# Heads of 64 rows: one head on each half of the array's rows, into two banks, in place of keys on a diagonal with zeros

## The chip, the cores and the metric

One core of one Trainium2 chip. The metric is the device time of one execution in microseconds (us), as the median of several runs.

## The reference

A stack of two networks on 256 tokens of width 1024, all in float32. The first has two layers: a mixer (layer 0, "even": two attentions of 8 heads of 64; layer 1, "odd": 8 differential heads, each of two score maps over 64 features), a cross attention to a memory of 256 tokens with 4 heads of 64 ("mem"), and a gated feed-forward. The second has two layers of feed-forward, a mixer of three branches ("mix"), and feed-forward again. The branches are a neighborhood attention with 8 heads of 64, a gated linear attention with 4 heads of 64 keys, and a latent attention whose heads have 128 + 64 features. What the change touches is the products that sum over 64 features or over a chunk of 64 tokens:

```python
s = jnp.einsum('bqhd,bkhd->bhqk', qb, k).astype(jnp.float32) * scale   # d = 64
p = masked_softmax(s, ...)
o = jnp.einsum('bhqk,bkhd->bqhd', p.astype(v.dtype), v)
...
a = jnp.where(tri, jnp.einsum('bhnid,bhnjd->bhnij', qe, ke), 0.0)      # gated linear, d = 64
upd = jnp.einsum('bhncd,bhncv->bhndv', k_end, v)                       # c = a chunk of 64 tokens
```

## The kernel before

The tokens are two tiles of 128 (t = 0, 1). Weights stream from HBM in pieces of 128x1024 (`raw`), are split into a high and a low part by ScalarE and VectorE (`split`, L390 and L392) and multiply in three single-pass products (`mm3`, L399 to L401). The feed-forwards take most of the time and are not touched.

In the attentions the two heads of a pair p lie on the 128 rows of `qT[:, p]`, 64 each. `kpair` (two copies for a tile) writes the keys of the first head into rows 0 to 63 of a buffer `kb[:, p, 0]` and those of the second into rows 64 to 127 of `kb[:, p, 1]`; the other halves were set to zero by `begin` or `mem_slots` on GpSimd. One matmul over all 128 rows (L686) gives the scores of both heads side by side in one PSUM bank `ps_s`:

```python
mm(o, qT[:, p, q], kb(p)[:, :, :w], start=True, stop=not mask)
```

A float32 matmul is two passes on TensorE in the trace: one written instruction is two in the counts. `causal_units` cuts the attention into units of one or two pairs; a unit fills one of the two banks of `ps_s`. After a unit come the largest value (L626, VectorE), the exponential (L636, ScalarE), the division (L643), the transposes (L455, into `ps_t`), the copy to `PT`, and the product with the values, which has 64 output columns for a head, so that the two heads of a pair stand on the two halves of the array's columns (L858, L885, L1082, L1246).

The gated linear attention has the same zeros: in `vb` (values, one chunk on each half, L1415) and `kb` (keys of the two directions, L1439). The latent attention adds the 64 further features of two heads by L1325.

The order on each engine is fixed when the kernel is built, by a scheduler that fills the gaps of an attention with the projections that come next. An engine then works through its list in order. A `with self.chain()` block takes its transposes into `ps_t`; work outside takes `ps_u`. In `mem` the projection of the queries of a tile also takes a bank of `ps_s`.

Of the kernel before, what the change touches and what calls it, by code (L numbers as in the profile page):

```python
# [50 lines left out]
BUFS = {"tok": (3, 2), "half": (3, 2), "xn": (2, 1), "P": (3, 3), "PT": (3, 3)}  # L51
# [83 lines left out]
def pack_rpb(rpb):  # L135

    tok = np.arange(256)
    r, c = tok // 64, tok % 64
    c0 = np.clip(c - 8, 0, 48)
    ok = (c[None, :] >= c0[:, None]) & (c[None, :] < c0[:, None] + 16)  # L140
    dr = np.broadcast_to(r[None, :] - r[:, None] + 7, (256, 256))
    dc = np.where(ok, c[None, :] - c[:, None] + 15, 31)
    padded = np.full((8, 15, 32), NEG, np.float32)
    padded[:, :, :31] = rpb
    return np.ascontiguousarray(padded[:, dr, dc].reshape(4, 2, 2, 128, 256).transpose(0, 2, 3, 1, 4))
# [56 lines left out]
class Net:  # L202
# [67 lines left out]
    def begin(self, na, nr, nk=()):  # L270
# [4 lines left out]
        self.K = [self.slot("slot", F32).rearrange("p (a b n) -> p a b n", a=4, b=2) for _ in nk]  # L275
# [4 lines left out]
        for k, n in zip(self.K, nk):  # L280
            nc.gpsimd.memset(k[0:64, :n, 1], 0.0)
            nc.gpsimd.memset(k[64:128, :n, 0], 0.0)
# [373 lines left out]

    def flat(self, P):
        return P.rearrange("p n w -> p (n w)")
# [7 lines left out]
    def kpair(self, kb, k0, v, t):  # L666

        m = v.shape[1]
        s = slice(t * 128, t * 128 + v.shape[2])
        for i in range(2):  # L670
            h = slice(i * 64, (i + 1) * 64)
            self.evac(kb[h, k0:k0 + m, i, s], v[h])

    def causal_units(self):

        return [(0, 128, (0, 1)), (0, 128, (2, 3))] + [(1, 256, (p,)) for p in range(4)]

    def score_unit(self, unit, qT, kb, extra=None, mask=True):
# [3 lines left out]
        S = self.bank("s").rearrange("p (n w) -> p n w", w=w)  # L682
        q = slice(t * 128, (t + 1) * 128)
        for i, p in enumerate(prs):
            o = S[:, 2 * i:2 * i + 2]
            mm(o, qT[:, p, q], kb(p)[:, :, :w], start=True, stop=not mask)  # L686
            if extra:
                extra(o, p, w)
            if mask:
                mm(o[:, :, w - 128:], self.identb, self.causal[:, None, :].to_broadcast([128, 2, 128]), start=False,  # L690
                   stop=True)
        return S[:, :2 * len(prs)]
# [84 lines left out]
    def even(self, xT, finish, filler):  # L777
# [5 lines left out]
        kb2, kb = self.K  # L783
# [3 lines left out]
        def evk(t, ps):  # L787
            self.rope(hd(kk[t][:, 0:384]), hd(ps[:, 0:384]), t, 6)
            self.evac(kk[t][:, 384:416], ps[:, 384:416])
            self.kpair(kb2, 0, self.transposes(kk[t][:, 128:384], 2), t)  # L790
# [7 lines left out]
        with self.chain():  # L798
# [11 lines left out]
            nc.vector.tensor_scalar(fl, fl, 0.0, None, op0=ALU.min)  # L810
            for i in range(2):
                nc.vector.tensor_sub(self.lfm[:, :, i, i::2], fl[:, :, i::2], fa[:, :, i::2])
# [8 lines left out]
            for t in range(2):  # L821
# [17 lines left out]
                for u in self.causal_units():  # L839
# [3 lines left out]
                    PTs = []  # L843
                    for br in range(2):
                        S = self.score_unit(u, qT2, lambda p: kb2[:, br])
                        P, r = self.softmax(S)
                        r2 = self.sm(r.shape[-1])
                        nc.vector.tensor_mul(r2, r, gt[:, t, 8 + 8 * br + 2 * prs[0]:8 + 8 * br + 2 * prs[-1] + 2])
                        self.scaled(P, r2)
                        PTs.append(self.probsT(self.flat(P)))  # L850
                    for i, p in enumerate(prs):
                        for h in range(2):
                            o = O[h * 64:h * 64 + 64, p]
                            mm(o, self.vcbd[:, 2 * p + h], PcT[:, 0], start=True, stop=False)
                            for br in range(2):
                                for b in range(t + 1):
                                    c = 128 + br * 128 + h * 64
                                    mm(o, v5[:, b, c:c + 64], PTs[br][:, (2 * i + h) * (t + 1) + b], start=False,  # L858
# [5 lines left out]
        for j in range(2):  # L864
            self.projT(st, xT, lambda c, ps: self.kpair(kb, 2 * j + c, ps[:, None, :], 0))
# [6 lines left out]
        with self.chain():  # L872
            O = None
            for u in self.causal_units():
                t, w, prs = u
                S = self.score_unit(u, qT, lambda p: kb[:, p], bias)
                P, r = self.softmax(S)
                self.scaled(P, r)
                PT = self.probsT(self.flat(P))
                if prs[0] == 0:  # L880
                    O = self.bank("o").rearrange("p (k n) -> p k n", k=4)
                for i, p in enumerate(prs):
                    for h in range(2):
                        for b in range(t + 1):
                            mm(O[h * 64:h * 64 + 64, p], V[:, b, p * 128 + h * 64:p * 128 + h * 64 + 64],  # L885
                               PT[:, (2 * i + h) * (t + 1) + b], start=b == 0, stop=b == t)
# [77 lines left out]
    def odd(self, xT, finish, filler):  # L964
# [14 lines left out]
        for half in range(2):  # L979
            kb = self.K[half]  # L980
            qT = self.q4(2 * half)
            def evk(t, ps):
                tk = self.tile([128, 512], F32, "tok")
                self.rope(hd(tk), hd(ps), t, 8)
                self.kpair(kb, 0, self.transposes(tk, 4), t)
# [7 lines left out]
            with self.chain():  # L993

                units = self.causal_units()
                for i, (ua, ub) in enumerate(zip(units[::2], units[1::2])):
                    t = ua[0]
                    Pd = self.tile([128, 4, 128], F32, "tok").rearrange("p a b -> p (a b)")
                    for j, u in enumerate((ua, ub)):
                        w, prs = u[1:]  # L1000
                        P, r = self.softmax(self.score_unit(u, qT, lambda p: kb[:, p]))
                        r2 = self.sm(r.shape[-1])
                        nc.vector.tensor_scalar(r2, r, self.lamc, None, op0=ALU.mult)
                        for p in range(len(prs)):
                            a, b = P[:, 2 * p], P[:, 2 * p + 1]
                            d = Pd[:, j * 256 + p * w:j * 256 + (p + 1) * w]
                            nc.vector.tensor_scalar(b, b, r2[:, 2 * p + 1:2 * p + 2], None, op0=ALU.mult)
# [539 lines left out]
```

## Time and profile before

| | us |
|---|---|
| median of 3 runs | 2085.9 (2081.1 to 2088.89) |
| the profiled execution: its time / its span | 2088.63 / 2086.9 |
| TensorE busy in the span | 2032.0 |
| VectorE, ScalarE, GpSimd busy | 1401.0, 1175.3, 106.5 |
| mean granted TensorE clock | 0.993 of full |

The span runs from the first to the last instruction; 1.7 us lie around it. TensorE's busy time counts a matmul from its start to its end, also while the next one already streams, so the distance from one start to the next is what a matmul costs.

### The profile page before, as it was taken

Reading aid. Unit: us, or ns where it says so; the run is one execution under the profiler, and the core shown is the slowest. Engines: PE = TensorE matmul, PEld = TensorE weight load, DVE = VectorE, ACT = ScalarE, POOL = GpSimd, SP = SyncE. Lnnn points to the kernel's source line nnn. Section 1 sums busy time; section 2 is a strip of 40 time slices with the busy share of each in tenths; the row PEclk is TensorE's granted clock in tenths of the full one; section 3 lists DMA queues with packets and bytes.
Section 4 is the critical chain, followed back from the end, with each engine's and each line's share of the span. In section 5 each row is a group of like instructions: output and inputs, shape, how many; then the busy total and the mean of one; then the engine's idle time right before and its main releaser. Section 6 shows DMA issues by size and latency. Waiting matters only on the chain.

```text
span 2086.9 us, 30850 instructions
## 1 busy us (share of the span) xinstructions
PE 2032.0 (97%) x11094; PEld 1703.5 (82%) x11094; DVE 1401.0 (67%) x2909; ACT 1175.3 (56%) x2566; POOL 106.5 (5%) x189
## 2 busy tenths in 40 slices
PE   7998999999899999999999999999999999999999
PEld 6866888877688889887778888888888878889887
DVE  7766766578676667665768677666665677867663
ACT  6645665466465556554654557555654564556652
POOL 1000000100100000002101000000000200100000
PEclk9999999999999999999999999999999999999999
DMA  7505565443456546553443467554663444556650
GB/s 239 173 30 182 175 229 182 144 142 116 167 187 225 184 142 228 186 182 109 151 165 122 157 202 253 191 183 161 217 189 111 147 153 136 172 175 206 225 182 31
DMA packets 100473, 352.15 MB, mean 169 GB/s; under 512 B 12468, under 2 KB 12980, under 8 KB 100320
## 3 DMA queue, kind: packets, MB, share of 16 engines
q1 hardware_dynamic: 96912, 337.99, 49.6%
q0 software_dynamic: 3408, 12.20, 1.9%
q8 instruction: 87, 1.43, 0.3%
q14 instruction: 66, 0.54, 0.1%
HBM read 349.09 MB, written 1.05 MB: 168 GB/s over the span
## 4 chain that ended last, share of the span: by engine, by line
PE 90%; DVE 3%; DMA 3%; ACT 2%; issue 1%; POOL 0%; ACTq 0%; DVEq 0%
PE ps_a L401 11%; PE ps_a L399 10%; PE ps_a L400 10%; PE ps_s L410 8%; PE ps_s L408 5%; PE ps_o L399 4%; PE ps_o L401 4%; PE ps_o L400 4%; PE ps_u L410 4%; PE ps_t L410 4%; PE ps_s L401 3%; PE ps_s L399 2%; PE ps_s L400 2%; PE ps_u L408 2%; PE ps_t L408 2%; PE ps_s L686 2%
## 5 line engine op out<-in xcount | busy, mean ns | idle before, releaser
L392 DVE TENSOR_TENSOR ring<-raw,ring 128x512 fp32r<-128x512 f32 x724 | 466.4, 679 | 165.5 <-ACT ring L390 159.7
L390 ACT ACTIVATE ring<-raw 128x512 fp32r<-128x512 f32 x724 | 411.8, 617 | 191.1 <-PE ps_a L401 69.8
L392 DVE TENSOR_TENSOR slot<-raw,slot 128x512 fp32r<-128x512 f32 x548 | 356.0, 687 | 187.2 <-ACT slot L390 185.2
L390 ACT ACTIVATE slot<-raw 128x512 fp32r<-128x512 f32 x548 | 314.2, 622 | 165.9 <-PE ps_o L401 108.1
L399 PE MATMUL ps_a<-ring,XX 128*128 128x512 f32 (+3 forms) x544 | 213.2, 395 | 3.8 <-ACT XX L390 3.8
L400 PE MATMUL ps_a<-ring,XX 128*128 128x512 f32 (+3 forms) x544 | 212.9, 392 | 0.0
L401 PE MATMUL ps_a<-ring,XX 128*128 128x512 f32 (+3 forms) x544 | 212.5, 391 | 0.0
L410 PE MATMUL ps_s<-XX,slot 128*128 128x512 f32 x492 | 178.1, 393 | 0.0
L408 PE MATMUL ps_s<-XX,slot 128*128 128x256 f32 x552 | 145.5, 281 | 0.0
L399 PEld LDWEIGHTS ps_a<-ring,XX 128*128 128x128 f32 x544 | 102.7, 190 | 25.7 <-ACT XX L390 5.6
L401 PEld LDWEIGHTS ps_a<-ring,XX 128*128 128x128 f32 x544 | 103.1, 190 | 22.2 <-issue 4.0
L400 PEld LDWEIGHTS ps_a<-ring,XX 128*128 128x128 f32 x544 | 103.3, 190 | 19.7 <-issue 1.4
L408 PEld LDWEIGHTS ps_s<-XX,slot 128*128 128x128 f32 x552 | 103.7, 188 | 6.7
L410 PEld LDWEIGHTS ps_s<-XX,slot 128*128 128x128 f32 x492 | 92.4, 188 | 18.7
L410 PE MATMUL ps_s<-XX,ring 128*128 128x512 f32 x264 | 96.1, 393 | 0.0
L410 PE MATMUL ps_t<-XX,slot 128*128 128x512 f32 x258 | 93.3, 393 | 0.0
L432 POOL TENSOR_TENSOR sm<-sm,mhalf 128x1 f32<-128x1 f32 (+2 forms) x72 | 59.1, 822 | 655.7 <-DVE sm L429 355.8
L410 PE MATMUL ps_u<-XX,slot 128*128 128x512 f32 x234 | 84.2, 393 | 0.0
L399 PE MATMUL ps_s<-slot,XX 128*128 128x256 f32 x288 | 81.8, 285 | 2.3 <-ACT XX L390 2.3
L401 PE MATMUL ps_s<-slot,XX 128*128 128x256 f32 x288 | 81.9, 288 | 0.0
L400 PE MATMUL ps_s<-slot,XX 128*128 128x256 f32 x288 | 81.1, 283 | 0.0
L408 PE MATMUL ps_s<-XX,ring 128*128 128x256 f32 x312 | 79.8, 281 | 0.0
(442 smaller groups left out, 4726.5 us busy)
## 6 DMA issues: line engine op xcount, KB each, us to landing
raw<-f SPq DMA_DIRECT2D x264, 512.0 KB, 4.3
raw<-ffn SPq DMA_DIRECT2D x132, 512.0 KB, 4.4
raw<-win SPq DMA_DIRECT2D x52, 512.0 KB, 4.2
raw<-wgt SPq DMA_DIRECT2D x48, 512.0 KB, 4.2
raw<-od_in SPq DMA_DIRECT2D x24, 512.0 KB, 4.2
raw<-wbr SPq DMA_DIRECT2D x24, 512.0 KB, 3.4
raw<-ev_in SPq DMA_DIRECT2D x16, 512.0 KB, 4.5
raw<-wout SPq DMA_DIRECT2D x16, 512.0 KB, 4.0
```

Of the source, the lines that this page charges most:

```text
L390: a = nc.scalar.activation(hi, src, AF.Copy, scale=scale)
L392: b = nc.vector.tensor_tensor(lo, src, hi.bitcast(F32), op=ALU.subtract)
L399: mm(out, a[0], b[0], start=first, stop=False)
L400: mm(out, a[0], b[1], start=False, stop=False)
L401: mm(out, a[1], b[0], start=False, stop=last)
L408: mm(out[:, :256], w[1], self.XX[:, k, 0], start=False, stop=False)
L410: mm(out, w[0], self.XX[:, k], start=False, stop=last)
L432: self.pow = nc.gpsimd.tensor_tensor(r, v, self.mhalf[:, :n], op=ALU.pow).ins
L686: mm(o, qT[:, p, q], kb(p)[:, :, :w], start=True, stop=not mask)
```

## The change

A matmul now takes one head: 64 rows of queries and 64 rows of keys, on the upper half of the array's rows for the first head and on the lower half for the second. The two heads go to two banks of `ps_s`. A unit therefore holds both banks, has twice as many pairs, and softmax runs over a bank of one head. The key buffers lose their zeros and are copied once. The gated linear attention and the latent attention change in the same way. `mem` takes its query projection into `ps_a` or `ps_o`. The buffers `P` and `PT` grow from 3 and 3 to 4 and 5, for which a DMA scratch area is made smaller.

```diff
-BUFS = {"tok": (3, 2), "half": (3, 2), "xn": (2, 1), "P": (3, 3), "PT": (3, 3)}
+BUFS = {"tok": (3, 2), "half": (3, 2), "xn": (2, 1), "P": (4, 4), "PT": (5, 5)}
...
+    def probs(self, Ss, biases=(None, None)):
+
+        PTs = []
+        for S, bias in zip(Ss, biases):
+            P, r = self.softmax(S, bias)
+            self.scaled(P, r)
+            PTs.append(self.probsT(self.flat(P)))
+        return PTs
...
     def causal_units(self):
 
-        return [(0, 128, (0, 1)), (0, 128, (2, 3))] + [(1, 256, (p,)) for p in range(4)]
+        return [(0, 128, (0, 1, 2, 3)), (1, 256, (0, 1)), (1, 256, (2, 3))]
 
-    def score_unit(self, unit, qT, kb, extra=None, mask=True):
+    def score_unit(self, unit, qT, kT, extra=None, mask=True):
...
-        S = self.bank("s").rearrange("p (n w) -> p n w", w=w)
+        n = len(prs)
+        S = [self.bank("s")[:, :n * w].rearrange("p (n w) -> p n w", w=w) for _ in range(2)]
         q = slice(t * 128, (t + 1) * 128)
         for i, p in enumerate(prs):
-            o = S[:, 2 * i:2 * i + 2]
-            mm(o, qT[:, p, q], kb(p)[:, :, :w], start=True, stop=not mask)
+            for h in range(2):
+                r = slice(h * 64, h * 64 + 64)
+                mm(S[h][:, i], qT[r, p, q], kT(p)[r, :w], start=i == 0 or not mask, stop=not mask)
...
+    def weigh(self, O, V, PTs, prs, nb, c0=0):
+
+        for i, p in enumerate(prs):
+            for h in range(2):
+                for b in range(nb):
+                    c = c0 + p * 128 + h * 64
+                    self.nc.tensor.matmul(O[h * 64:h * 64 + 64, p], V[:, b, c:c + 64], PTs[h][:, i * nb + b], start=b == 0,
+                                          stop=b == nb - 1)
...
-                ps = self.bank("s")[:, :256]
+                ps = self.bank("ao"[t])[:, :256]
...
-                        U = self.bank("o").rearrange("p (h c v) -> p h c v", h=2, c=2)
-                        for j in range(2):
-                            h = 2 * g + j
-                            mm(U[:, j], E[:, h * 128:h * 128 + 128], vb[:, h, :, tq(t)], start=True, stop=True)
+                    U = [self.bank("o").rearrange("p (h v) -> p h v", h=4) for _ in range(2)]
+                    for h in range(4):
+                        hs = slice(h * 128, h * 128 + 128)
+                        for c in range(2):
+                            r = slice(c * 64, c * 64 + 64)
+                            mm(U[c][:, h], E[r, hs], V[r, t, hs], start=True, stop=True)
```

The scheduler's order moves with it. On TensorE, in the second attention of the even mixer (tile t = 1), a unit of one pair stood before as one matmul for both heads (`ps_s_167`) with its mask (L690):

```order
L401 MATMUL ps_a_319_1692<-ring_308_1659,slot_37_198 128x512
L686 MATMUL ps_s_167_911<-slot_38_199,slot_30_191 128x512
L690 LDWEIGHTS identb_216
L690 MATMUL ps_s_167_911<-causal_228,identb_216 128x2x128
L858 MATMUL ps_o_118_725<-PT_134_780,slot_30_191 64x128
```

and stands now as two stretches, `ps_s_158` of the first head and `ps_s_159` of the second, each with the two pairs and a mask (L692), with projections (L395 to L397) between them:

```order
L686 MATMUL ps_s_158_886<-slot_34_195,slot_30_191 128x256 x2
L692 LDWEIGHTS identb_211
L692 MATMUL ps_s_158_886<-causal_223,identb_211 128x2x128
L396 MATMUL ps_a_318_1699<-ring_305_1659,slot_38_199 128x512
L397 MATMUL ps_a_318_1699<-ring_305_1659,slot_38_199 128x512
...
L686 MATMUL ps_s_159_887<-slot_34_195,slot_30_191 128x256 x2
L692 LDWEIGHTS identb_211
L692 MATMUL ps_s_159_887<-causal_223,identb_211 128x2x128
```

The two heads no longer stand next to each other. In the first `mem` the scores of tile 1 stood on TensorE behind the twelve matmuls of the output projection of tile 0 (`ps_a_420` and `ps_a_421`; the last two of them here):

```order
L400 MATMUL ps_a_421_2149<-ring_401_2063,slot_393_2034 128x512
L401 MATMUL ps_a_421_2149<-ring_401_2063,slot_393_2034 128x512
L686 MATMUL ps_s_444_2238<-slot_40_213,slot_391_2032 128x512
L686 MATMUL ps_s_451_2261<-slot_40_213,slot_391_2032 128x512
L455 MATMUL ps_t_449_2250<-identf_88,P_445_2240 128x128 x4
```

and stand now behind two of them, with the heads in turn (`ps_s_443`, `ps_s_444`) and ten of the twelve still to come:

```order
L395 MATMUL ps_a_419_2155<-ring_398_2061,slot_392_2039 128x512
L396 MATMUL ps_a_419_2155<-ring_398_2061,slot_392_2039 128x512
L686 MATMUL ps_s_443_2245<-slot_39_209,slot_390_2037 128x256
L686 MATMUL ps_s_444_2246<-slot_39_209,slot_390_2037 128x256
L686 MATMUL ps_s_443_2245<-slot_39_209,slot_390_2037 128x256
L686 MATMUL ps_s_444_2246<-slot_39_209,slot_390_2037 128x256
L397 MATMUL ps_a_419_2155<-ring_398_2061,slot_392_2039 128x512
```

The scores moved ahead by ten matmuls. On VectorE at the same place the division of the first probabilities (`P_445`, L643) stood behind the norm of tile 0's output (L489, L490):

```order
L626 TENSOR_REDUCE sm_446_2241<-ps_s_444_2238 128x2
L489 SCALAR_TENSOR_TENSOR xn_428_2172<-ps_a_420_2148,sm_427_2169,slot_392_2033 128x512
L489 SCALAR_TENSOR_TENSOR xn_429_2175<-ps_a_421_2149,sm_427_2169,slot_392_2033 128x512
L490 TENSOR_TENSOR x_73<-x_73,xn_428_2172 128x512
L638 RECIPROCAL sm_448_2243<-sm_447_2242 128x2
L626 TENSOR_REDUCE sm_453_2264<-ps_s_451_2261 128x2
L490 TENSOR_TENSOR x_73<-x_73,xn_429_2175 128x512
L643 TENSOR_SCALAR P_445_2240<-P_445_2240,sm_448_2243 128x256 x2
```

and both divisions (now L639) stand ahead of it (now L485, L486):

```order
L639 TENSOR_SCALAR P_445_2251<-P_445_2251,sm_448_2254 128x256 x2
L388 TENSOR_TENSOR ring_493_2398<-raw_492_2396,ring_493_2398 128x512
L425 SCALAR_TENSOR_TENSOR sm_425_2175<-sm_421_2169,sm_423_2172 128x1
L634 RECIPROCAL sm_454_2271<-sm_453_2270 128x2
L639 TENSOR_SCALAR P_451_2268<-P_451_2268,sm_454_2271 128x256 x2
L485 SCALAR_TENSOR_TENSOR xn_427_2179<-ps_a_419_2155,sm_426_2176,slot_391_2038 128x512
```

The norm moved behind the softmax of the next tile.

## Rows read from the trace of the kernel before

**Rows 1.** The page: span, and busy time of TensorE (share, instructions).

```profile
span 2086.9 us, 30850 instructions
PE 2032.0 (97%) x11094; PEld 1703.5 (82%) x11094; DVE 1401.0 (67%) x2909; ACT 1175.3 (56%) x2566; POOL 106.5 (5%) x189
```

**Rows 2.** The page's chain that ended last, by engine.

```profile
PE 90%; DVE 3%; DMA 3%; ACT 2%; issue 1%; POOL 0%; ACTq 0%; DVEq 0%
```

**Rows 3.** Stretches: start:end, length, busy us of each engine, clock (PEclk), DMA.

```profile
185.00:217.00 32.00, 23.42 (x128) 17.36 (x130) 20.76 (x46) 16.26 (x48) 2.96 (x5) 0.85 0.23 79
...
535.00:588.00 53.00, 39.45 (x204) 30.27 (x204) 34.17 (x71) 26.77 (x72) 5.57 (x11) 0.87 0.29 92
960.00:1215.00 255.00, 252.30 (x1310) 203.80 (x1309) 181.68 (x408) 143.95 (x301) 28.56 (x41) 1.00 0.47 152
```

**Rows 4.** TensorE's groups by shape (rows*columns of the array, operand): the scores.

```profile
L686 PE MATMUL ps_s<-slot,slot 128*128 128x512 f32 x88 | 45.4, 609 | 3.7 <-DVE slot L1071 2.5 <-ACT P L636 1.1
...
L686 PE MATMUL ps_s<-slot,slot 128*128 128x256 f32 x40 | 11.8, 390 | 0.0
```

**Rows 5.** Timeline of TensorE around a product on column halves: start, busy us.

```profile
1685.64 0.40 PE L400 MATMUL ps_a<-ring,XX 128*128 128x512 f32 x1
1685.96 0.66 PE L1246 MATMUL ps_o<-PT,slot 128*64 128x128 f32 x8
1686.56 0.66 PE L455 MATMUL ps_t<-identf,P 128*128 128x128 f32 x4
1687.05 1.02 PE L686 MATMUL ps_s<-slot,slot 128*128 128x512 f32 x2
1687.91 0.38 PE L455 MATMUL ps_u<-identf,half 128*128 128x128 f32 x2
```

**Rows 6.** Timeline of TensorE around a product over 33 rows (33*128).

```profile
1061.60 0.40 PE L400 MATMUL ps_a<-ring,XX 128*128 128x512 f32 x1
1061.92 1.12 PE L1351 MATMUL ps_u<-slot,gT 33*128 33x512 f32 x2
1062.97 0.50 PE L401 MATMUL ps_a<-ring,XX 128*128 128x512 f32 x1
1063.31 0.39 PE L399 MATMUL ps_a<-ring,XX 128*128 128x512 f32 x1
1063.54 0.40 PE L400 MATMUL ps_a<-ring,XX 128*128 128x512 f32 x1
```

**Rows 7.** Timeline of TensorE in the first mem, tile 1.

```profile
206.62 1.88 PE L686 MATMUL ps_s<-slot,slot 128*128 128x512 f32 x4
212.04 1.09 PE L455 MATMUL ps_t<-identf,P 128*128 128x128 f32 x4 [3.54 <-DVE P L643]
```

**Rows 8.** The chain at that place: start, us, what.

```profile
208.36 1.41 DVE xn L489 x2
...
211.62 0.28 DVE P L643
```

**Rows 9.** Timeline of TensorE in the second mem, tile 0.

```profile
557.31 1.96 PE L686 MATMUL ps_s<-slot,slot 128*128 128x512 f32 x4 [1.26 <-DVE slot L1071]
...
561.38 0.63 PE L455 MATMUL ps_t<-identf,P 128*128 128x128 f32 x4 [1.68 <-DVE P L643]
```

**Rows 10.** The same, tile 1.

```profile
569.67 1.88 PE L686 MATMUL ps_s<-slot,slot 128*128 128x512 f32 x4
...
574.18 0.63 PE L455 MATMUL ps_t<-identf,P 128*128 128x128 f32 x4 [0.33 <-DVE P L643]
```

**Rows 11.** The chain at the odd mixer's end.

```profile
526.36 8.03 DMA raw<-memq
...
540.62 0.43 PE ps_o L399
```

**Rows 12.** Timeline of TensorE there.

```profile
539.53 1.08 PE L455 MATMUL ps_t<-identf,tokA 128*128 128x128 f32 x4 [4.46 <-DVE tokA L976]
```

**Rows 13.** The scores' line: what TensorE waited for (us, times).

```profile
  ACT P L636: 2.6, 4
```

More of the change, by code (lines that the diff above doesn't have):

```diff
@@ L842, in even @@
                     w, prs = u[1:]
-                    PTs = []
+                    PTs = [[], []]
                     for br in range(2):
[L845 to L850, printed above, removed]
+                        for h, S in enumerate(self.score_unit(u, qT2, lambda p: kT2[:, br])):
+                            P, r = self.softmax(S)
+                            r2 = self.sm(r.shape[-1])
+                            c = 8 + 8 * br + 2 * prs[0] + h
+                            nc.vector.tensor_mul(r2, r, gt[:, t, c:c + 2 * len(prs) - 1:2])
+                            self.scaled(P, r2)
+                            PTs[br].append(self.probsT(self.flat(P)))
                     for i, p in enumerate(prs):
@@ L875, in even @@
                 t, w, prs = u
[L876 to L879, printed above, removed]
+                PTs = self.probs(self.score_unit(u, qT, lambda p: kT[:, p], bias))
                 if prs[0] == 0:
                     O = self.bank("o").rearrange("p (k n) -> p k n", k=4)
[L882 to L886, printed above, removed]
+                self.weigh(O, V, PTs, prs, t + 1)
                 if prs[-1] == 3:
@@ L1237, in na @@
             O = self.bank("o").rearrange("p (k n) -> p k n", k=4)
-            for p in range(4):
-                S = self.score_unit((t, 256, (p,)), qT, lambda p: kb[:, p], mask=False)
-                P, r = self.softmax(S, self.ins[f"rpb{l}"][p, t])
-                self.scaled(P, r)
-                PT = self.probsT(self.flat(P))
-                for h in range(2):
-                    for b in range(2):
-                        c = p * 128 + h * 64
-                        mm(O[h * 64:h * 64 + 64, p], V[:, b, c:c + 64], PT[:, 2 * h + b], start=b == 0, stop=b == 1)
+            for i in range(2):
+                prs = (2 * i, 2 * i + 1)
+                S = self.score_unit((t, 256, prs), qT, lambda p: kT[:, p], mask=False)
+                self.weigh(O, V, self.probs(S, self.ins[f"rpb{l}"][i, t]), prs, 2)
             s = slice(t * 128, (t + 1) * 128)
@@ L1434, in gla @@
             As.append(A)
-            for g in range(2):
-                ps = self.bank("s").rearrange("p (h e i) -> p h e i", h=2, e=2)
-                for i in range(2):
-                    for e in range(2):
-                        mm(ps[:, i, e], kb[:, 2 * g + i, e, tq(t)], qeT[:, 2 * g + i, tq(t)], start=True, stop=True)
-                tmp = self.tile([128, 512], F32, "tok").rearrange("p (h e i) -> p h e i", h=2, e=2)
-                nc.vector.tensor_mul(tmp, ps, self.tri[:, None, 0:2].to_broadcast([128, 2, 2, 128]))
-                nc.vector.tensor_add(A[:, 2 * g:2 * g + 2], tmp[:, :, 0], tmp[:, :, 1])
+            parts = [self.bank("s").rearrange("p (h i) -> p h i", h=4) for _ in range(2)]
+            for h in range(4):
+                for e in range(2):
+                    r = slice(e * 64, e * 64 + 64)
+                    mm(parts[e][:, h], keT[r, h, tq(t)], qeT[r, h, tq(t)], start=True, stop=True)
+            tmp = self.tile([128, 4, 128], F32, "tok")
+            for e, dst in enumerate((tmp, A)):
+                nc.vector.tensor_mul(dst, parts[e], self.tri[:, None, e].to_broadcast([128, 4, 128]))
+            nc.vector.tensor_add(A, A, tmp)
         for t, A in enumerate(As):
@@ L1464, in run @@
         self.load(stages[0][2], self.stream(first[0]), first[1])
-        self.mkb, self.mV = {}, {}
-        kinds = {"even": (4, 4, (2, 4)), "odd": (4, 3, (4, 4)), "mem": (2, 1), "mix": (4, 3, (4, 4, 4))}
+        self.mkT, self.mV = {}, {}
+        kinds = {"even": (5, 4), "odd": (5, 3), "mem": (2, 1), "mix": (6, 3)}
         names = [s[0] for s in stages]
```

179 lines of the change are left out of this document (74 added, 105 removed).

## The prediction

> **What bounds the kernel now.** I read the page first. TensorE is busy for 2032.0 of 2086.9 us [rows 1], and the chain that ended last runs through it for 90% [rows 2]. The other engines matter only where TensorE stands still. The windows tell where that is: in the long attention of the second network it is busy 252.30 of 255.00 us, so there a microsecond of TensorE is a microsecond of the kernel; in the two memory attentions it is busy 23.42 of 32.00 and 39.45 of 53.00 us, and the mean granted clock is 0.85 and 0.87 [rows 3]. The change therefore has two accounts: TensorE's time in the mixers, one for one, and the waits in `mem`, where order counts.
>
> **What the streaming costs.** A head pair of 256 keys is 512 columns in two passes. In the timeline two passes start at 1687.05 and the next work at 1687.91, so a pass of 512 columns costs 0.86 / 2 = 0.43 us [rows 5], 256 columns 0.215 and 128 columns 0.107. (The 609 ns of the groups [rows 4] are start to end and overlap.) All scores stay the same number of columns: before, 512 columns with half the multiplied rows zero; now 256 for each head. Nothing is saved unless the two halves of the rows stream at the same time. The order has 39 places where four half-height passes of 256 columns could lie beside four others, each worth 4 x 0.215 = 0.86, in all 39 x 0.86 = 33.5 us.
>
> **Do halves overlap?** For the halves of the columns yes: L1246 issues eight passes of 128 columns, which one behind the other would be 8 x 0.107 = 0.85, and the next instruction starts 0.60 later (1685.96 to 1686.56) [rows 5]. With one stretch per half and an entry and exit this is what two streams give. For halves of the rows no row shows it; before has only single products over 33 rows. The bounds are 0 (one after the other) and the whole half. I take the whole, since the column halves come near it.
>
> **Where the heads stand next to each other.** In the order after, they alternate in 18 of the 39 places: 4 in `mem`, 2 first units of odd, 2 first units of the neighborhood attention, 4 in the latent attention, and 6 of the gated linear (4 of U at L1397, 2 of A). There the overlap can work: 18 x 0.86 = 15.5 us saved. In the other 21 (even 9, odd 4, neighborhood 6, gated linear 2) the scheduler has put projections, or nothing but one head, between them, as the front shows for `ps_s_158` and `ps_s_159`: no gain.
>
> The Trainium skill, page "TensorEngine Tiling (Array Packing)", section Theoretical Speedup, gives up to 2x for a contraction of at most 64. By it the sum would hold 33.5 in place of 15.5 us. No row here shows a row-half pair, and the column pair above reaches 0.85 / 0.60.
>
> **What a stretch of halves costs.** Around the product over 33 rows: the whole-array matmul before it starts at 1061.60 and the product at 1061.92, 0.32 in place of the 0.23 between two of that kind (1063.31 to 1063.54); the product's two passes hold the engine for 1.05 (1061.92 to 1062.97) where two of 0.43 are 0.86; the next matmul takes 0.34 (1062.97 to 1063.31) in place of 0.23. Together 0.09 + 0.19 + 0.11 = 0.39 us for going in and out [rows 6]. The entry to column halves costs the same 0.09 (1685.64 to 1685.96) [rows 5], so it is the change of shape that costs. Counted in the two orders, TensorE changes between whole array and halves 136 times before and 228 after, mostly 59 new score stretches less 7 value stretches that merge. That is 92 / 2 = 46 round trips, 46 x 0.39 = +17.9 us. Lower bound: only the 0.19 inside, 46 x 0.19 = 8.7. I take 17.9, since the row has all three parts.
>
> **What the values lose.** `weigh` (new L702) writes head after head within a pair. The first head's `PT` is ready earlier, so in 8 neighborhood units and 2 of the second `mem` the first matmuls run for one half alone. Four passes of 128 columns lose their partner in each: 10 x 4 x 0.107 = +4.3 us; 0 if the scheduler's list still pairs them. I take 4.3.
>
> **The memory attentions.** Part of the 4 x 0.86 = 3.4 saved there falls into waits of TensorE; I count half of it as lost, +1.7 (0 to 3.4). Then the order. In the first `mem`, tile 1, the scores start at 206.62 and the transposes wait 3.54 for the division, until 212.04 [rows 7]; the chain shows why: the norm of the tile before (L489, 1.41 us) stands on VectorE ahead of the division at 211.62 [rows 8]. In the order after, the scores start ten matmuls earlier (10 x 0.23 = 2.3), and the division stands ahead of the norm. In the second `mem`, where both were so already, scores to transposes is 569.67 to 574.18, 4.5 us, with a wait of 0.33 [rows 10]. So the transposes come at about 206.62 - 2.3 + 4.5 = 208.8, where they came at 212.04, and the ten matmuls fill the time between. Of the wait of 3.54, the 0.33 and a little more should stay: I take -3.1 (0 if the norm, now late, delays tile 0's transposes for the feed-forward by as much). In the second `mem`, tile 0, the transposes wait 1.68 [rows 9]; the projection of the next queries no longer needs a bank of `ps_s`, and twelve of its matmuls of 256 columns, 12 x 0.12 = 1.4 us, move in: -1.4 (0 to -1.68).
>
> **The odd mixer's end.** TensorE waits 4.46 there [rows 12], and the chain leads back to a weight transfer from memory of 8.03 us that began at 526.36 [rows 11], which the change doesn't touch. The odd mixer's own increase, 11 round trips x 0.39 - 2 x 0.86 = 2.6, is in the sum and disappears in this wait if the transfer starts no later: -2.0 (0 to -2.6).
>
> **Off the path.** VectorE has 2911 to 2880 instructions in the order, ScalarE 2332 to 2313, and GpSimd loses 16 large memsets. They are busy 1401.0, 1175.3 and 106.5 us [rows 1]: 0. TensorE's work hides this; without that cover it would be a gain, by 1401.0 us / 2909 = 0.48 us for each of VectorE's 31 fewer, 15 us. SP's 675 instructions only change places by a few, the bias transfers of the neighborhood against `raw`: 0. The new wait is the second head's stretch for its bank, which now must be empty of a whole earlier unit; behind it on TensorE stand projections (L395 to L397), which nothing needs soon. I count 0; the bound is in the second rival.
>
> **Sum.** +17.9 - 15.5 + 4.3 + 1.7 - 3.1 - 1.4 - 2.0 = +1.9 us. The profiled execution took 2088.63, so it becomes 2090.5; it stood 2.7 above the median of 2085.9, which becomes 2088. About 0.5% (10.4 us) is what a measurement of this kernel can tell from no change.
>
> **The rivals.**
> *Row halves don't overlap* (0.14). For it: no row shows the overlap. Against: the column halves. The -15.5 and the +1.7 go: +13.8, 2102, slower. The point from which it decides: with under four tenths of the overlap, the time is over 2096.
> *The second head waits for its bank* (0.10). Both banks of `ps_s` belong to one unit, so no unit's scores stand ahead of the softmax of the one before. Before, TensorE waited for the exponential at the scores 4 times, 2.6 us, 0.65 each [rows 13]. For 14 of some 40 separated stretches: 14 x 0.65 = +9, 2097. Against: the scheduler has projections to put there; it decides from 13 waits on.
> *The waits of `mem` go* (0.14). TensorE stands 8.6 + 13.6 = 22.2 us in the two windows [rows 3]; 6.5 of this is in my sum. Behind the long wait [rows 12] a pass takes 0.43 in place of 0.23 [rows 11], the lower of the two clock levels, 1.2 and not 2.4 GHz. The lower level costs (1 - 0.85) x 32 + (1 - 0.87) x 53 = 11.7 us of work at most. Half of the 15.7 left and a third of this: -12, 2076, at the edge of faster.
> *All of it overlaps* (0.05): 39 x 0.86 in place of 18 x 0.86, -18.0, 2070, faster. TensorE would have to stream the heads of the 21 other places together; the order shows projections between them. The rule of the page named above ends here.
>
> **The numbers.** My forecast has 0.57, and by itself the range 2081 to 2095: round trips at 0.19 take 9 off, the terms of `mem` and odd at nothing put 6.5 on. The whole range reaches from just under the third rival, 2074, to the first, 2102. Faster: the fourth and half of the third, 0.13. Slower: the first, most of the second and a tail of the forecast, 0.23. The rest, 0.64, is the same within 0.5%.
>
> **What would show it.** Right: in the 18 places, matmuls of 64 rows that start in pairs almost together, and a pair that costs half; 0.3 to 0.4 us lost around each stretch of halves; the wait at the first `mem`'s transposes down to under 0.5 us, with a higher clock in that window; TensorE's whole busy time nearly unchanged. Wrong: halves that start one after the other at 0.215; long waits for L632 (the exponential) in front of L686; L702 no slower than L1246 and L1082 were; waits in `mem` that appear at the norm (L485) instead. The forecast fails most easily by the price of a round trip, which rests on products over 33 rows alone.

## The result and the profile after

The changed kernel takes 2104.6 us (median of 4 runs, 2100.82 to 2107.19) against 2085.94: 1.009 times as long, interval 1.0064 to 1.0116. It is slower by 0.9%, and over the top of the range. The profiled execution after took 2100.82 us, before 2088.63. So 12.2 us of the 18.7 between the medians can be followed in the two traces. The rest lies between executions of the same kernel: of the four runs after, the two with a mean granted clock of 0.994 took 2100.8 and 2102.7 us, the two with 0.990 and 0.991 took 2107.2 and 2106.5.

The page of the kernel after, its span and busy times, to be held against [rows 1]:

```profile
span 2099.1 us, 31060 instructions
PE 2036.3 (97%) x11244; PEld 1707.1 (81%) x11244; DVE 1389.0 (66%) x2878; ACT 1168.3 (56%) x2547; POOL 88.6 (4%) x173
```

The first subtraction to make is span less busy time of TensorE. Before it is 2086.9 - 2032.0 = 54.9 us, after 2099.1 - 2036.3 = 62.8. Of 12.2 us more, 4.3 are work and 7.9 are standing still. Its windows, as in [rows 3]:

```profile
185.00:217.00 32.00, 22.73 (x139) 17.24 (x138) 20.63 (x45) 17.23 (x50) 2.31 (x4) 0.88 0.32 107
...
535.00:588.00 53.00, 38.82 (x212) 30.29 (x210) 35.27 (x73) 27.12 (x69) 5.38 (x10) 0.91 0.42 139
960.00:1215.00 255.00, 252.18 (x1335) 202.65 (x1334) 172.85 (x392) 137.49 (x289) 24.68 (x37) 1.00 0.45 142
```

In the windows of the memory attentions the granted clock is a little higher. But the second kernel crosses a window of fixed times later, by all that came before, so what is gained or lost there can't be read from it, and the waits have to be read one by one. The timeline of TensorE after shows both sides of the account (start, busy us, [wait, and what ended it]):

```profile
206.06 0.40 PE L396 MATMUL ps_a<-ring,slot 128*128 128x512 f32 x1
206.39 1.13 PE L686 MATMUL ps_s<-slot,slot 64*128 64x256 f32 x8
207.45 0.50 PE L397 MATMUL ps_a<-ring,slot 128*128 128x512 f32 x1
207.79 0.40 PE L395 MATMUL ps_a<-ring,slot 128*128 128x512 f32 x1
...
210.49 0.63 PE L451 MATMUL ps_t<-identf,P 128*128 128x128 f32 x4 [0.48 <-DVE P L639]
212.42 0.87 PE L702 MATMUL ps_o<-PT,slot 128*64 128x128 f32 x4 [1.30 <-ACT PT L412]
...
215.91 1.97 PE L702 MATMUL ps_o<-PT,slot 128*64 128x128 f32 x12 [1.56 <-DVE PT L414]
...
226.67 0.39 PE L395 MATMUL ps_s<-slot,XX 128*128 128x256 f32 x1 [0.81 <-ACT slot L386]
...
549.89 1.09 PE L451 MATMUL ps_t<-identf,tokA 128*128 128x128 f32 x4 [7.33 <-DVE tokA L983]
...
1018.67 1.13 PE L686 MATMUL ps_s<-slot,slot 64*128 64x256 f32 x4
1019.73 0.43 PE L395 MATMUL ps_a<-ring,XX 128*128 128x352 f32 x1
...
1228.28 0.66 PE L451 MATMUL ps_u<-identf,slot 128*128 128x128 f32 x4 [1.72 <-DVE slot L390]
```

Eight passes of 256 columns, two heads in turn, hold the engine from 206.39 to 207.45, 1.06 us. Four passes of one head hold it from 1018.67 to 1019.73, 1.06 as well. So the second head is free where it stands next to the first, and costs the whole again where it does not.

The waits by what ended them (us in all, times, longest), after:

```profile
...
PE ps_t L451 <- DVE tokA L983: 7.3, 1, 7.3
PE ps_t L451 <- DVE P L639: 5.1, 5, 2.4
PE ps_o L702 <- DVE PT L414: 5.0, 5, 1.6
...
PE ps_u L451 <- DVE slot L390: 3.4, 2, 1.7
PE ps_o L702 <- ACT PT L412: 3.1, 2, 1.8
...
PE ps_a L702 <- ACT PT L412: 0.7, 1, 0.7
```

and the same before, where nothing waits for L394, the line that is L390 after:

```profile
PE ps_t L455 <- DVE P L643: 8.0, 5, 3.5
...
PE ps_t L455 <- DVE tokA L976: 4.5, 1, 4.5
...
PE ps_o L1082 <- ACT PT L416: 3.0, 2, 2.3
...
PE ps_o L1246 <- ACT PT L416: 2.4, 2, 1.2
...
PE ps_o L1082 <- DVE PT L418: 0.8, 1, 0.8
```

The wait for the division (`P`) fell by 2.9. In its place stand waits for the copies of `PT` (8.8 in place of 6.2), for the odd mixer's last norm (`tokA`, +2.8), and at the ends of the two mix stages (+3.4): together +5.9 of the 7.9.

### The profile page after: what moved, and what is told of

Its sections match the earlier page's. It is cut to its first block, busy times and chain, and to the rows that moved or that the text cites. A ratio compares the mean times of both kernels' runs of the same rounds, so it can differ in the third digit from the quotient of the medians.

```text
span 2099.1 us, 31060 instructions
## 1 busy us (share of the span) xinstructions
PE 2036.3 (97%) x11244; PEld 1707.1 (81%) x11244; DVE 1389.0 (66%) x2878; ACT 1168.3 (56%) x2547; POOL 88.6 (4%) x173
## 4 chain that ended last, share of the span: by engine, by line
PE 89%; DVE 5%; DMA 2%; ACT 2%; issue 1%; POOL 0%; SPq 0%; ACTq 0%; DVEq 0%; POOLq 0%
PE ps_a L395 10%; PE ps_a L397 10%; PE ps_a L396 10%; PE ps_s L406 8%; PE ps_s L404 5%; PE ps_o L395 4%; PE ps_o L397 4%; PE ps_o L396 4%; PE ps_u L406 4%; PE ps_t L406 4%; PE ps_u L404 2%; PE ps_t L404 2%; PE ps_s L397 2%; PE ps_s L395 2%; PE ps_s L396 2%; PE ps_s L686 2%
## 5 line engine op out<-in xcount | busy, mean ns | idle before, releaser
L395 PE MATMUL ps_a<-ring,XX 128*128 128x512 f32 (+3 forms) x560 | 216.6, 390 | 6.0 <-ACT XX L386 4.7
L397 PE MATMUL ps_a<-ring,XX 128*128 128x512 f32 (+3 forms) x560 | 216.6, 387 | 0.2 <-DVE XX L388 0.2
L396 PE MATMUL ps_a<-ring,XX 128*128 128x512 f32 (+3 forms) x560 | 214.7, 384 | 0.1
L395 PEld LDWEIGHTS ps_a<-ring,XX 128*128 128x128 f32 x560 | 105.9, 189 | 29.5 <-ACT XX L386 6.7
L397 PEld LDWEIGHTS ps_a<-ring,XX 128*128 128x128 f32 x560 | 105.9, 189 | 23.1 <-issue 3.9
L396 PEld LDWEIGHTS ps_a<-ring,XX 128*128 128x128 f32 x560 | 106.1, 189 | 19.1 <-DVE ring L388 0.8
L406 PEld LDWEIGHTS ps_s<-XX,slot 128*128 128x128 f32 x492 | 92.4, 188 | 18.7
L395 PE MATMUL ps_s<-slot,XX 128*128 128x256 f32 x288 | 81.9, 285 | 3.8 <-ACT XX L386 3.0
L397 PE MATMUL ps_s<-slot,XX 128*128 128x256 f32 x288 | 81.9, 288 | 0.1
```

The lines of the kernel that those rows point to most:

```text
L395: mm(out, a[0], b[0], start=first, stop=False)
L396: mm(out, a[0], b[1], start=False, stop=False)
L397: mm(out, a[1], b[0], start=False, stop=last)
L406: mm(out, w[0], self.XX[:, k], start=False, stop=last)
```

## The experiments

Twelve kernels, each beside runs of the kernel before on the same chip. Ratios are to the kernel before.

| | us | ratio (interval) | before on that chip |
|---|---|---|---|
| e1 heads held together | 2103.17 | 1.0085 (1.0071 to 1.0099) | 2085.2 |
| e2 new units, whole rows | 2098.01 | 1.0061 (1.0048 to 1.0073) | 2085.2 |
| e3 earlier splits | 2106.55 | 1.0102 (1.0087 to 1.0118) | 2085.2 |
| e4 norm ahead again | 2103.47 | 1.0088 (1.0074 to 1.0102) | 2085.2 |
| e5 memory attentions alone | 2088.31 | 1.0012 (1.0003 to 1.002) | 2086.06 |
| e6 even and odd alone | 2094.22 | 1.0037 (1.0024 to 1.005) | 2086.06 |
| e7 mix alone | 2093.8 | 1.0032 (1.0022 to 1.0042) | 2086.06 |
| e8 buffers alone | 2085.8 | 1.0001 (0.9993 to 1.001) | 2086.06 |
| e9 linear and latent alone | 2086.11 | 0.9998 (0.9989 to 1.0006) | 2085.8 |
| e10 the same, held together | 2089.6 | 1.0022 (1.0013 to 1.003) | 2085.8 |
| e11 neighborhood alone | 2089.68 | 1.0024 (1.0014 to 1.0034) | 2085.8 |
| e12 odd alone | 2091.37 | 1.0031 (1.0022 to 1.0041) | 2085.8 |

**e1, all heads side by side.**

```diff
+        gate = [mm(s[:, 0, :1], self.identb, self.identb[:, :1], start=True, stop=True).ins for s in S]
+        with self.after(*gate):
             for i, p in enumerate(prs):
                 for h in range(2):
...
```

> All 39 places now have both heads in turn: before each unit two one-column matmuls of the identity, one into each bank, hold the scores back until both banks are free (62 of them; the order has 200 changes between whole array and halves instead of 228). Theory A (two accounts: TensorE's own work is about even, and waits at the stage joints make the loss): the joints stay, so the 12 to 19 us of loss lose only the streaming of the 21 separated places, 21 x 0.86 = 18, and 28 changes x 0.2 = 5.5, less about 62 x 0.06 = 4 for the one-column matmuls: about 2085. Theory B (holding back the first head costs the softmax behind it as much time as the streaming saves): 2100 or more, with new waits at the transposes of the attentions.

Measured 2103.17: no gain worth the name over the changed kernel. The page says why:

```profile
span 2104.1 us, 31173 instructions
PE 2029.7 (96%) x11306; PEld 1705.1 (81%) x11306; DVE 1389.1 (66%) x2878; ACT 1167.6 (55%) x2547; POOL 93.4 (4%) x173
```

TensorE's work fell by 2036.3 - 2029.7 = 6.6 us although the granted clock of this execution was 0.988, not 0.994 (in the four runs 0.988 to 0.991, in those of the change 0.990 to 0.994). Its standing time rose from 62.8 to 74.4. The streaming that the separated places had not given is to be had, and holding back the first head costs as much. Theory B has the time right and the place wrong: the wait for the division at the transposes hardly grew (5.4 us for 5.1), and the new waits are spread over many lines, the largest growth at one of them being 2.2 us.

**e2, the new units without row halves.** Keys with zeros again, the two banks kept. The lines are held against the changed kernel; the gated linear and the latent attention, too, are here as in the kernel before:

```diff
-                r = slice(h * 64, h * 64 + 64)
-                mm(S[h][:, i], qT[r, p, q], kT(p)[r, :w], start=i == 0 or not mask, stop=not mask)
+                mm(S[h][:, i], qT[:, p, q], kT(p)[:, h, :w], start=i == 0 or not mask, stop=not mask)
```

> The units, the two banks, the order of the softmax and of the values as in the change for both causal mixers, the memory attention and the neighborhood attention, but each head's scores again over 128 rows against keys with zeros (the gated linear and the latent attention as in the kernel before). No row halves, so no overlap and no entry or exit for scores. Theory A (the waits come from the new units and order, not from the halves): the waits at the odd mixer's end (7.33) and in the first memory attention stay; 2094 to 2102. Theory C (the halves themselves are the loss, 46 round trips of 0.4 us): 2086 to 2090.

Measured 2098.01, as theory A had it: 12.8 us of loss with no row half in the scores. Page and timeline of this kernel:

```profile
span 2098.4 us, 31070 instructions
PE 2037.0 (97%) x11212; PEld 1728.5 (82%) x11212; DVE 1401.2 (67%) x2903; ACT 1175.1 (56%) x2566; POOL 107.4 (5%) x189
```

```profile
206.81 1.89 PE L688 MATMUL ps_s<-slot,slot 128*128 128x256 f32 x8
208.35 0.58 PE L401 MATMUL ps_a<-ring,slot 128*128 128x512 f32 x1
208.77 0.39 PE L399 MATMUL ps_a<-ring,slot 128*128 128x512 f32 x1
...
211.25 0.63 PE L455 MATMUL ps_t<-identf,P 128*128 128x128 f32 x4 [0.23 <-DVE P L643]
213.18 0.65 PE L713 MATMUL ps_o<-PT,slot 128*64 128x128 f32 x4 [1.30 <-ACT PT L416]
...
216.66 1.72 PE L713 MATMUL ps_o<-PT,slot 128*64 128x128 f32 x12 [2.25 <-DVE PT L418]
...
545.96 1.09 PE L455 MATMUL ps_t<-identf,tokA 128*128 128x128 f32 x4 [5.38 <-DVE tokA L994]
```

The waits of the changed kernel are there in the memory attention and in the odd mixer: little before the transposes, 1.30 and 2.25 before the values, 5.38 at the odd mixer's end. Those for L394 at the ends of the mix stages are not. The scores themselves take 208.77 - 206.81 - 0.23 = 1.73 us for two pairs on whole rows, the 0.23 being the one projection among them. TensorE works 2037.0 and stands 61.4. From the kernel before to this one that is +5.0 and +6.5; from this one to the change, -0.7 and +1.4, with the gated linear and the latent attention in the difference.

**e3, earlier splits in the odd mixer.**

```diff
-    "odd": "346888899999aabb",
+    "odd": "1246666777778899",
```

> Only the table is changed that says behind which point of the odd mixer each piece of the output weights is split: two points earlier. Theory A: the points of the table now come later, since one unit holds the softmax of both heads, so that the splits, and the buffer that the transfer of the next weights waits for, are late; with earlier splits the transfer starts about 9 us earlier, and the wait at the odd mixer's end falls from 7.33 to about 4: 2101. Theory C (the stretches of halves alone): the wait only moves, 2104 to 2106.

Measured 2106.55, just over what theory C gave. The issue of the transfers on SP's queue stood in the kernel before at

```profile
523.48 3.21 SPq L365 DMA_DIRECT2D raw<-memq  x2
```

after the change at

```profile
533.26 2.52 SPq L361 DMA_DIRECT2D raw<-memq  x2
```

and here, 5.9 us earlier than after the change, at

```profile
527.37 1.53 SPq L361 DMA_DIRECT2D raw<-memq  x2
```

but TensorE waits in two places instead of one, 4.74 for the norm of the next stage's input and 1.25 for the odd mixer's own:

```profile
546.84 0.95 PE L451 MATMUL ps_u<-identf,xn 128*128 128x128 f32 x4 [4.74 <-DVE xn L470]
549.03 1.09 PE L451 MATMUL ps_t<-identf,tokA 128*128 128x128 f32 x4 [1.25 <-DVE tokA L983]
```

The transposes come at 549.03 where they came at 549.89. So the late transfer was no more the limit than the chain of softmax, values and norms that ends beside it; theory A's reason for this wait fell.

**e4, the norm ahead of the division again, in the first memory attention.** `wait` is the last addition of tile 0's norm, and is given for tile 1 of the first `mem` alone:

```diff
-            self.scaled(P, r)
+            with self.after(*wait):
+                self.scaled(P, r)
```

> Only in the first memory attention: the divisions of tile 1 stand on VectorE behind the norm of tile 0 again, as in the kernel before. Theory A (the wait before the transposes was only moved behind the norm): the wait at the transposes comes back, the waits behind it (1.30, 1.56 and those at the start of the feed-forward) go: within 1.5 us of the changed kernel, 2103 to 2106. Rival (putting the softmax ahead of the norm is itself the loss here, about 4 us): 2100. My prediction's step (softmax ahead saves 3 us): 2108.

Measured 2103.47, within the 1.5 us. The whole wait is again in front of the transposes:

```profile
215.26 1.09 PE L451 MATMUL ps_t<-identf,P 128*128 128x128 f32 x4 [5.30 <-DVE P L639]
```

Behind it only 0.69 is left. By the medians either order of the two on VectorE costs the same within the noise.

**e5 to e8, the parts by themselves.** Each is the kernel before with the functions of one part exchanged; e8 exchanges none:

```diff
-BUFS = {"tok": (3, 2), "half": (3, 2), "xn": (2, 1), "P": (3, 3), "PT": (3, 3)}
+BUFS = {"tok": (3, 2), "half": (3, 2), "xn": (2, 1), "P": (4, 4), "PT": (5, 5)}
...
-    nc = bacc.Bacc("TRN2", target_bir_lowering=False, num_devices=1)
+    nc = bacc.Bacc("TRN2", target_bir_lowering=False, num_devices=1, dynamic_dma_scratch_size=8192)
```

> The kernel before, with the two memory attentions alone changed (and the larger P and PT). Theory A (small losses at many joints): the overlap there saves 4 x 0.86 of TensorE, of which the waits give back most: 2084 to 2089. Rival D (the memory attentions carry most of the loss): 2095 or more.

> The kernel before, with the even and the odd mixer alone changed (and the larger P and PT). Theory A: about 2092, of it 3 at the odd mixer's end, where the wait of 4.46 grows. Rival E (the two causal mixers carry it all): 2100 or more.

> The kernel before, with the three branches of the two mix stages alone changed (and the larger P and PT). Theory A: the two mix stages were 3.6 and 3.2 longer in the profiled execution, so 2092 to 2094. Rival (the overlap that half of their places have pays there): 2086 or less.

> The kernel before, with nothing changed but the number of buffers of P and PT (4 and 5 in place of 3 and 3) and the smaller DMA scratch area. Theory A: no change, 2084 to 2088. Rival F (the smaller scratch area or the moved buffers slow transfers): 2090 or more.

The buffers change nothing (rival F falls). The three parts lose 2.2, 8.2 and 7.7 us against the kernel before on that chip, 18.1 in all, where the whole change loses 18.7. No single place carries it (D and E fall), and the parts add up within their intervals.

**e9 to e12, parts of parts.** Again the functions of one part alone; e10 adds for A what e1 adds for the scores:

```diff
+            gate = [mm(s[:, 0, :1], self.identb, self.identb[:, :1], start=True, stop=True).ins for s in parts]
+            with self.after(*gate):
                 for h in range(4):
                     for e in range(2):
...
```

> The kernel before, with the gated linear and the latent attention alone changed (neighborhood attention as before), so mostly places where the heads stand next to each other. From the trace of the change, four passes of 256 columns for each head side by side take 1.06 us, plus 0.1 at the entry and 0.1 at the exit, where the whole array took 1.72: -0.45 for such a place; a head alone takes the same 1.06 + 0.2, so a place with its heads apart costs +0.8. Theory G (adjacent places gain, separated ones lose): a layer has -0.45 for U, -0.9 for the latent scores, -1.3 for the second U and A that stand in one stretch, +0.8 for the first A, whose halves stand apart: -1.8, 2082. Rival A (the units of one head cost waits there too): 2086 to 2090.

> As the run before, and A's two halves held together by one-column matmuls into both banks. Theory G: U, A and the latent scores each -0.45 at six places of a layer, +0.4 for the one-column matmuls: -2.3 for a layer, 2081. Rival A: new waits in front of the held matmuls, 2086 to 2090.

> The kernel before, with the neighborhood attention alone changed. Theory G: of its four units in a layer one has the heads in turn (-0.45) and three have them apart (+2.5), and the values, which begin with one head alone, lose 4 x 0.43 = 1.7: +3.7 for a layer, 2093. Rival (its units are long enough to hide it): 2086 to 2088.

> The kernel before, with the odd mixer alone changed. Theory A: most of the 8.2 us that the even and the odd mixer lost together, since the wait at its end grows: 2090 to 2092. Theory G (only the separated places count; here 4 of 6, +0.8 each, less 2 x 0.45): 2088.

e9's page, and its timeline at the end of the first mix stage:

```profile
span 2084.4 us, 30872 instructions
PE 2025.8 (97%) x11126; PEld 1694.3 (81%) x11126; DVE 1393.2 (67%) x2891; ACT 1173.6 (56%) x2558; POOL 98.6 (5%) x185
```

```profile
1210.81 0.60 PE L455 MATMUL ps_u<-identf,slot 128*128 128x128 f32 x4
...
1216.03 0.66 PE L455 MATMUL ps_u<-identf,slot 128*128 128x128 f32 x4 [1.78 <-DVE slot L394]
```

and the same transposes in the kernel before:

```profile
1210.03 0.66 PE L455 MATMUL ps_u<-identf,slot 128*128 128x128 f32 x4
...
1217.17 0.60 PE L455 MATMUL ps_u<-identf,slot 128*128 128x128 f32 x4
```

TensorE works 6.2 us less than before (1.8 of it in each of the two mix stages, as theory G had summed; the rest lies in stages that e9 leaves as they were), and stands 58.6 - 54.9 = 3.7 more, of it the wait of 1.78 at the end of a mix stage, which the kernel before does not have. Between the two groups of transposes TensorE has 26 matmuls in the kernel before and nine in e9: in the order that the scheduler built, the other 17 moved ahead of the first group, and the wait for the split of the second tile (L394 on VectorE) is no longer covered. The median is that of the kernel before, as rival A had it. e10 makes it worse, 2089.6, with more waiting (its span of 2089.0 - 2027.9 = 61.1), in rival A's range again:

```profile
PE 2027.9 (97%) x11134; PEld 1697.1 (81%) x11134; DVE 1392.4 (67%) x2891; ACT 1172.5 (56%) x2558; POOL 103.0 (5%) x185
```

e11 lost 3.9, about half of what G summed for it and more than its rival gave. e9 and e11 together lose 4.2 by the medians, e7 with both 7.7; the intervals overlap. e12 lost 5.6, as much as A said, but not by A's reason:

```profile
span 2090.3 us, 30894 instructions
PE 2037.8 (97%) x11122; PEld 1708.3 (82%) x11122; DVE 1398.7 (67%) x2901; ACT 1174.1 (56%) x2564; POOL 102.6 (5%) x186
```

TensorE works 5.8 more and stands 52.5, less than before, and the wait at the odd mixer's end fell to 2.5. All of the 5.8 lies in the odd mixer, where the mean granted clock is 0.95 in place of 0.98; (0.98 - 0.95) x 151 = 4.5 us of it can be the clock (an estimate from that stage's length). With a clock of 0.98 there the changed kernel works 1.3 more. So e12's time lies in the range of theory A, and its cause is open.

**The stages in all the traces.** Eight instructions of TensorE that every kernel has cut its trace into stages (in the kernel before they start at 0, 189.56, 410.41, 555.62, 600.12, 776.49, 1229.46 and 1882.06; the stretch from 600.12 to 776.49 is the same in all). The table has its lengths in us: the range over the kernels that leave the stage as it was, the range over those that have the change in it (the change, e1, e3, e4 and the parts e5 to e7 and e12; e2 and e9 to e11 change a stage only in part), and three kernels by themselves:

| stage | unchanged | changed | the change | e1 | e2 |
|---|---|---|---|---|---|
| up to the first `mem` | 189.6 to 194.4 | 191.0 to 195.6 | 191.2 | 195.6 | 190.8 |
| first `mem`, feed-forward | 219.5 to 221.1 | 221.9 to 224.9 | 223.5 | 224.1 | 224.4 |
| odd mixer | 143.0 to 145.7 | 146.6 to 151.8 | 150.6 | 146.6 | 146.9 |
| second `mem` | 41.9 to 45.6 | 42.3 to 46.1 | 42.3 | 45.9 | 47.1 |
| feed-forward, first mix | 452.0 to 453.1 | 454.8 to 456.6 | 456.6 | 454.8 | 454.3 |
| feed-forward, second mix | 651.8 to 653.1 | 655.5 to 657.2 | 655.8 | 657.2 | 655.6 |

Two stages scatter by as much as anything changes in them, so no pair of traces says what happened there: the one up to the first `mem`, and the second `mem`. In the other four the loss is clear of the scatter. There TensorE is busy and stands (us, us; the granted clock is 0.98 in the first two stages and 1.00 in the mix stages, in each of these traces):

| stage | before | the change | e2 | e9 | e11 |
|---|---|---|---|---|---|
| first `mem`, feed-forward | 211.7, 9.2 | 212.2, 11.3 | 213.1, 11.3 | | |
| odd mixer | 137.6, 7.7 | 138.8, 11.8 | 137.4, 9.5 | | |
| feed-forward, first mix | 450.3, 2.7 | 451.4, 5.2 | 451.6, 2.7 | 448.5, 4.8 | 453.1, 2.9 |
| feed-forward, second mix | 648.7, 3.9 | 650.0, 5.8 | 650.6, 5.1 | 646.9, 5.7 | 651.5, 3.4 |

The change works about 1 us more in each of the four, and stands 2 to 4 us more.

## Why the prediction was wrong

**Right: the halves of the rows.** They overlap fully where the heads alternate (1.06 us for both), and the four passes of a head alone take the same 1.06. The predicted price of a round trip, 0.39, is now readable in the changed kernel itself: the entry takes 0.33 in place of 0.23 (206.06 to 206.39), the inside 1.06 where four passes of 0.215 are 0.86, the exit 0.34 (207.45 to 207.79): 0.10 + 0.20 + 0.11 = 0.41. So a place of two pairs with the heads in turn takes 1.06 + 0.21 = 1.27 in place of 1.72 on whole rows (1.73 in e2), and one with the heads apart 2 x 1.27 = 2.54. The rule of the Trainium skill, page "TensorEngine Tiling (Array Packing)", section Theoretical Speedup, up to 2x for a contraction of at most 64, is not contradicted by the trace; here 1.72 / 1.27 is 1.35, since the entry and the exit count.

**Right in its terms, too high in sum: TensorE's work.** The terms for the streaming, the round trips and the values, with the 1.7 for the overlap not gained in `mem`, are 17.9 - 15.5 + 4.3 + 1.7 = 8.4. The page shows +4.3. That the halves give about what they take was the mechanism, and the mix stages bear it out: from e2, with whole rows, to the change TensorE's work moves by -0.2 and -0.6. The linear and the latent attention alone save 1.8 in each (e9), and the neighborhood attention alone takes 2.8 more in each (e11). The values can be read in the changed kernel:

```profile
1025.61 0.65 PE L702 MATMUL ps_o<-PT,slot 128*64 128x128 f32 x4
1026.19 1.13 PE L686 MATMUL ps_s<-slot,slot 64*128 64x256 f32 x4
...
1028.69 1.09 PE L702 MATMUL ps_o<-PT,slot 128*64 128x128 f32 x12 [0.78 <-DVE PT L414]
1029.71 0.38 PE L395 MATMUL ps_a<-ring,XX 128*128 128x256 f32 x1
```

Two pairs take 0.58 + 1.02 = 1.60 where they took two times 0.60 [rows 5], 0.40 more. Twelve units have this pattern, eight of the neighborhood attention and all four of `mem`, where the prediction counted ten: +4.8 at this price for its +4.3. Four of them, 1.6, lie in each mix stage, where e2 works 1.3 and 1.9 more than the kernel before.

**Wrong: the new units, put at nothing, and the waits.** Two steps failed. The first is in "Off the path": of the new units it has only the wait of the second head for its bank, and "I count 0". e2 has the units, the banks and the new order with no row half in the scores. Of the prediction's terms the +4.3 for the values and the -3.1 and -1.4 of `mem` apply to it, -0.2 in all; it lost 12.8. The second step is the one from "The memory attentions" to "The odd mixer's end": -3.1, -1.4 and -2.0, in all -6.5. TensorE's standing time rose by 7.9.
The -3.1 was right at its place: the wait before the transposes fell from 3.54 to 0.48, and they came at 210.49, 1.7 after the forecast 208.8, about as much as this stage starts later in this execution (1.6). But behind it stand 1.30, 1.56 and, in the feed-forward, 0.81. Behind the transposes of the kernel before there was

```profile
213.81 1.13 PE L1082 MATMUL ps_o<-PT,slot 128*64 128x128 f32 x8 [0.69 <-ACT PT L416]
```

and no wait at the other values. The prediction had named this end ("0 if the norm, now late, delays") and took the other. The stage is at least 0.8 us longer wherever it is changed (221.9 against 221.1), in the change 2.4. e4 shows by its median that the order on VectorE is worth nothing clear of noise; its stage, 221.9, is the shortest of the changed ones.
Of the -1.4 the wait shows 0.8 (from 1.68 to 0.86); the stage scatters too much to tell.
The -2.0 had a condition, that the transfer starts no later. It started later: its issue moved from 523.48 to 533.26, and the mixer itself began only 4.3 later. The wait grew from 4.46 to 7.33. The transfer is not all of it: in e3 it was issued 5.9 earlier, and the transposes came 0.9 earlier. In e12 the wait fell by the 2.0 that the prediction had, and the stage was 151.3, longer than in any kernel that leaves it unchanged (up to 145.7). So the term for this stage was mis-sized: +2.6 of work and -2.0 of waits were forecast, and the change works 1.3 more there and stands 4.1 more. With whole rows (e2) the stage stands 1.8 more, so over half of the 4.1 comes only with the row halves; by which way, no run separates.
The waits at the ends of the two mix stages, 1.7 each, were in no step. I had read those stages as windows in which TensorE never waits [rows 3]. e9 has these waits, and its mix stages are about as long as unchanged ones (453.3 and 652.6): what the linear and the latent attention save there, 1.8, is waited away, 2.1 and 1.8. e11 has none of them, and its stages are 3.0 and 2.3 longer than before: what the neighborhood attention takes more is paid one for one, as the prediction had it.

**The rivals.** "The second head waits for its bank" named the new units, which hold both banks, and its 2097 is what e2 took, but its place was wrong. The matmuls of the scores wait for no exponential in the changed kernel, which its groups by shape show (busy us, mean ns | idle, what ended it):

```profile
L686 PE MATMUL ps_s<-slot,slot 64*128 64x256 f32 x176 | 42.9, 402 | 1.3 <-DVE slot L1074 1.3
```

The view of [rows 13] counts weight loads beside the matmuls: of its 2.6 us, which the prediction took as four waits, 1.1 us in two are the matmuls' own [rows 4]; after the change it has one weight load, 0.4 us. What waits is behind the scores, the values and the norms. In e2 matmuls of the scores do wait for the exponential, twice, 2.4 us. e2 shows that the new units, banks and order lose 12.8 us, where the whole change loses 18.7, without any row half in the scores. "Row halves don't overlap" gave 2102, close to the time by luck: the timeline refutes its reason. "The waits of `mem` go" is refuted by e5, "all of it overlaps" by the four passes of a head alone, which take 1.06. Two figures of the prediction don't follow from its working, and nothing hangs on them: round trips at 0.19 give 2088 - 9 = 2079 for the lower end and not 2081, and the chance of faster, the fourth rival and half of the third, is 0.12.

**What stays open.** The last step from e2 (2098.0) to the change (2104.6) is 6.6 us between the medians and 0.7 between the profiled executions (2098.4 and 2099.1). Part of the 6.6 goes with the lower granted clock of two of the four runs of the change; why these runs have it, no experiment here tells. In the profiled executions the change is 3.7 longer than e2 in the odd mixer and 2.3 in the first mix, and 4.8 shorter in the second `mem`, which scatters that much. Which part of the new units makes the waits, that softmax runs head by head or that a unit fills both banks, was not separated. No version that I ran beats the kernel before.

## What to carry to other kernels

Cost a change of the array's shape by the stretch: here about 0.4 us for going in and out, which two heads of one stretch share and two stretches pay twice; count in the built order how many stand side by side before counting any overlap. When the heads are split over two banks, ask first what the coarser units do to the chain behind the scores: build the new units without the new matmul form, as e2 did, and see what is lost before anything can be won. And a wait that is removed in front of one instruction is only gained if nothing that was queued behind it becomes late; look two stages on. And before you explain a difference of one stage between two traces, see how long that stage is in kernels that leave it unchanged: here one of them scatters by 4.8 us.

## What the runs showed of the hardware

Both heads' halves stream entirely beside each other: 1.06 us for eight passes and 1.06 for four. The column halves had shown the same, for 0.60 us is four passes of 0.107 and 0.17 over, as 1.06 is four of 0.215 and 0.20 over. And an execution that works 6.6 us less can take as long: in e1 TensorE's work fell, its waits rose by 11.6 us, and the mean granted clock was 0.988 where the changed kernel's profiled execution had 0.994.
